# Low parts of seven weight units per layer on GpSimd, centring in another order, and gate tiles at a later place in a two-layer encoder kernel

## The chip, the cores and the metric

The kernel runs on one core of one Trainium2 chip. The metric is the device time of one execution in microseconds, the median of several runs.

## What is computed

A bidirectional encoder trunk of two layers over 256 tokens and 16 learned meta tokens of width 1024, in float32. Each layer projects the normalised tokens with one wide matrix, runs two token mixers on the parts, gates and mixes them, and ends in a squared-ReLU MLP:

```python
h = concat(meta_tokens, x)                                # 272 x 1024
for l in range(2):
    u = rms_norm(h, norm_mix_pre[l])
    q_r, k_r, v_r, g_r, q_a, k_a, v_a, gate_r, gate_a = split(u @ w_in[l])
    y_r = retention_branch(q_r, k_r, v_r, g_r, log_decay) @ w_ret_o[l]   # 8 heads, both directions
    y_a = attention_branch(q_a, k_a, v_a, attn_sink[l]) @ w_att_o[l]     # 8 query heads, 2 key heads
    mix = (sigmoid(gate_r) * y_r + sigmoid(gate_a) * y_a) @ w_mix_o[l]
    h = h + rms_norm(mix, norm_mix_post[l])
    u = rms_norm(h, norm_ff_pre[l])
    h = h + rms_norm(square(relu(u @ w_ff1[l])) @ w_ff2[l], norm_ff_post[l])
return h[:, 16:]
```

## The kernel before

The tokens lie along the free axis, 272 columns in layer 0 and 256 for most of layer 1. The weights come as 130 units per layer, each a tile `raw` of 128 x 1024 float32 loaded by one DMA on the SP queue into a ring of three buffers. `unit()` splits each one: ScalarE (ACT) writes the high part `wh` (L131, a copy to fp32r) and VectorE (DVE) the low part `wl = raw - wh` (L132). Both are kept in rings of four, so a unit is split some units before it is used. `mm3` (L136 to L138) then makes three fp32r matmuls for every 128 x 128 block: wh with the high part of the tokens, wh with their low part, wl with the high part. A unit is 24 matmuls, of some 126 ns each at 272 columns.

Units 4 to 18 of a layer bring the retention values v_r, one head each, the attention's key k_a, four q_a, v_a, and the first of the retention's q_r and k_r. In order: k_a is unit 6 in layer 0 (v_r of head 5 in layer 1), v_r of heads 6 and 7 are 8 and 10, v_a is 12, the four q_a lie at odd numbers around them, q_r and k_r at 14 to 18.

For each value head `value_r` has DVE scale the projection into `vt` (L424). GpSimd (POOL) copies the 16 meta tokens, four times over, into `pads` (L427), and later `centre()` runs on TensorE (PE): one matmul of `pads` for the meta tokens (L430, into `ps_s`) and two of `vt` for the 256 tokens (L432, into `ps_t`). These are deferred and so lie among the matmuls of the next unit. The attention's queries are rotated on DVE (L389 to L392, tile `t`), split into `qa` by ACT (L459) and DVE (L93), and in layer 0 their meta tokens are scaled into a block matrix on POOL (L465, tile `m`), from which L564 takes the meta scores. The values of the attention are copied into `vblk` by POOL (L484) and transposed on PE (L487, L488). Probabilities are scaled by POOL for the meta keys (L594, `pmk`) and by ACT for the others (`pn`, L596).

The retention heads come later in the layer. `similar(hh)` makes two score tiles per head (L680, L681) and multiplies them by the decay `tt` into `sd` (DVE); `retained(hh)` multiplies these with the values (L691) and the meta tokens' state (L692). `meta(t)` makes the `tmx` and `tm` tiles that L692 reads. Behind the first head DVE makes the gate tiles `gt` from `tg` in eight instructions (L720, L721).

Every engine works through its own queue in order. Which instruction comes when on a queue is set by the tile framework's scheduler, from the program's order and its own estimates; `tc.issue_after` adds a constraint that an instruction is issued behind a named one. A small helper records all `scalar_tensor_tensor` instructions, so these carry its line, L93. PE's queue is filled by a list of units (`fill`), with the rest placed between.

Of the kernel before, what the change touches and what calls it, by code (L numbers as in the profile page):

```python
# [22 lines left out]
T = SEQ + NM  # L23
# [4 lines left out]
UNITS = 46 + 4 + 8 + 8 + 32 + 32  # L28
TW = 400
ROW = 320  # L30
LAG = 4
F = [8, 9, 6, 6, 2, 7, 2, 5, 4]
BEHIND = 4
# [8 lines left out]
def encoder(ctx: ExitStack, tc: tile.TileContext, order, w, h_in, gains, dec, decm, sink, sinkm, tabs, mats, esel, masks, rel, relm, grow, out):  # L42
    nc = tc.nc
    V, A, PE, G = nc.vector, nc.scalar, nc.tensor, nc.gpsimd
    mul, add, sub, mn = ALU.mult, ALU.add, ALU.subtract, ALU.min
# [15 lines left out]
    def slot(i, name, shape=(KD, T), dt=F32):  # L61
        return big.tile([P] + list(shape), dt, tag=f"b{i}", name=name)
# [7 lines left out]
    def tokens(i, name, shape=(KD,), at=32):  # L70
        return slot(i, name, (*shape, ROW), F32R)[..., at:at + T]

    def bank(tag, shape=None):
        t = psum.tile([P, 512], F32, tag=tag, name="ps_" + tag, bufs=BANKS[tag])
        if shape is None:
            return t
        n = int(np.prod(shape))
        v = t[:, :n]
        if len(shape) == 2:
            v = v.rearrange("p (a b) -> p a b", a=shape[0])  # L80
        elif len(shape) == 3:
            v = v.rearrange("p (a b c) -> p a b c", a=shape[0], b=shape[1])
        return v
# [5 lines left out]
    def f(t):  # L89
        return t.bitcast(F32)  # L90

    def stt(o, a, s, b, op0=mul, op1=mul):
        V.scalar_tensor_tensor(out=o, in0=a, scalar=s, in1=b, op0=op0, op1=op1)  # L93

    def split(xh, xl, x):
        A.activation(xh, x, AF.Copy)  # L96
# [11 lines left out]
    def fetch(parts=1):  # L108
        i = count["load"]
        count["load"] += 1  # L110
        raw = ring.tile([P, D], F32, tag="raw", name="raw", bufs=3)
        n = D // parts
        cuts = [slice(j * n, (j + 1) * n) for j in range(parts)]
        raws.append((raw, cuts))
        for c in cuts:
            nc.sync.dma_start(raw[:, c], w[i][:, c])
            yield

    def unit(*name):
        i = len(order)  # L120
        order.append(name)
        if not raws:
            list(fetch())
        raw, cuts = raws.pop(0)
        wh = ring.tile([P, D], F32R, tag="wh", name="wh")
        wl = ring.tile([P, D], F32R, tag="wl", name="wl")
        for c in cuts:
            with ExitStack() as later:
                for ins in held.get(i, ()):
                    later.enter_context(tc.issue_after(ins))  # L130
                A.activation(wh[:, c], raw[:, c], AF.Copy)  # L131
                V.tensor_tensor(out=wl[:, c], in0=raw[:, c], in1=f(wh[:, c]), op=sub)  # L132
        return wh, wl

    def mm3(ps, ah, al, bh, bl, first=True, last=True):
        PE.matmul(ps, ah, bh, start=first, stop=False)  # L136
        PE.matmul(ps, ah, bl, start=False, stop=False)  # L137
        return PE.matmul(ps, al, bh, start=False, stop=last)  # L138
# [3 lines left out]
    def flush():  # L142
        while deferred:
            deferred.pop(0)()

    def product(x, c0, tag, *name):
        wh, wl = unit(*name)
        ps = bank(tag, [T])
        for k in range(KD):
            sl = slice(k * P, (k + 1) * P)  # L150
            ins = mm3(ps[:, c0:], wh[:, sl], wl[:, sl], x[0][:, k, c0:], x[1][:, k, c0:], k == 0, k == KD - 1)
            if k == LAG and deferred:
                with tc.issue_after(ins.ins):
# [3 lines left out]
    def proj(x, c0, tag, *name):  # L157
        for _, ps in product(x, c0, tag, *name):
            pass
        return ps  # L160
# [164 lines left out]
    mat = {}  # L325
# [12 lines left out]
    def fourfold(x):  # L338
        return x.unsqueeze(1).to_broadcast([x.shape[0], 4, 16])
# [23 lines left out]
    for l in range(DEPTH):  # L363
        c0 = 16 * l
# [51 lines left out]
        def value_r(hh):  # L416
            q, m = hh // 4, hh % 4
            if m == 0:
                tpv[q] = bank("s", [4, P]), [bank("t") for _ in range(2)]
            tpm, tps = tpv[q]  # L420
            vt = ready.get(hh)
            if vt is None:
                vt = two.tile([P, T], F32, tag="t1", name="vt")
                last = V.scalar_tensor_tensor(out=vt, in0=early.pop(0) if early else proj(u, 0, "a", "v_r", hh), scalar=-0.5, in1=rb, op0=mul, op1=mul)  # L424
                scaled.append(last.ins)
            mine = vtm[:, m]
            G.tensor_copy(mine[:, :, 16 * (m % 2):16 * (m % 2) + 16], fourfold(vt[:, 0:16]))  # L427

            def centre():
                PE.matmul(tpm[:, m], mine, mat["cen"], start=True, stop=True)  # L430
                for c in range(2):
                    PE.matmul(tps[c][:, m * P:(m + 1) * P], vt[:, 16 + c * P:16 + (c + 1) * P], mat["cen"], start=True, stop=True)  # L432
                if m == 3:
                    for c in range(2):
                        A.activation(vr[:, c, q * 512:(q + 1) * 512], tps[c], AF.Copy)
                    A.activation(vm[:, 4 * q:4 * q + 4], tpm, AF.Copy)
                    for r in odds:
                        low = vm[r, 4 * q:4 * q + 4]
                        V.tensor_tensor(out=low, in0=tpm[r], in1=f(low), op=sub)

            deferred.append(centre)
            if early:
                flush()
# [55 lines left out]
        gt = slot(4, "gt")  # L499
# [47 lines left out]
        def behind():  # L547
            return tc.issue_after(anchor[0])
# [12 lines left out]
        if l == 0:  # L561
            ps = bank("s")
# [5 lines left out]
            for c in range(4):  # L568
                V.tensor_tensor(
                    out=pmblk.rearrange("p (t c g k) -> p t c g k", t=4, c=4, g=2)[:, :, c],  # L570
                    in0=mat["blk"].rearrange("p (t g k) -> p t g k", t=4, g=2),
                    in1=pm[:, 0:16].unsqueeze(1).unsqueeze(1).to_broadcast([P, 4, 2, 16]),
                    op=mul,
# [72 lines left out]
        tg = slot(8, "tg")  # L646
# [21 lines left out]
        def similar(hh):  # L668
            gg, t = hh % 2, hh // 2
            tt = two.tile([P, TW], F32, tag="tt", name="tt")  # L670
            tb = two.tile([P, P], F32, tag="tb", name="tb")
            A.activation(tt[:, 144:], rel_sb[:, 0, 144:], AF.Exp, scale=de[:, l, 0, hh:hh + 1])
            A.activation(tt[:, :144], rel_sb[:, 1, :144], AF.Exp, scale=de[:, l, 1, hh:hh + 1])
            A.activation(tb, rel_sb[:, 1, 144:144 + P], AF.Exp, scale=de[:, l, 1, hh:hh + 1])
            V.tensor_tensor(out=tt[:, 144:144 + P], in0=tt[:, 144:144 + P], in1=tb, op=mul)
            sds[hh] = []
            for c in range(2):
                ps = bank("s")
                sl = slice(16 + c * P, 16 + (c + 1) * P)
                PE.matmul(ps[:, c0:T], qk[1][:, gg, t, sl], qk[0][:, gg, t, c0:], start=True, stop=False)  # L680
                PE.matmul(ps[:, c0:T], qk[1][:, gg, t, sl], ql[gg][:, t, c0:], start=False, stop=True)  # L681
                sd = four.tile([P, T], F32, tag="sd", name="sd")
                o = c0 + P - P * c
                stt(sd[:, c0:], ps[:, c0:T], 0.125, tt[:, o:o + T - c0])
                sds[hh].append(sd)

        def retained(hh):
            t = hh // 2
            po = pos[hh] = bank("ot"[hh % 2], [T])
            for c in range(2):  # L690
                PE.matmul(po[:, c0:], vr[:, c, hh * P:(hh + 1) * P], sds[hh][c][:, c0:], start=c == 0, stop=False)  # L691
            PE.matmul(po[:, c0:], vm[:, hh], tm[:, t, c0:], start=False, stop=True)  # L692
            pvs[hh] = square(po[:, c0:], c0)
# [19 lines left out]
        for hh in range(8):  # L713
            with behind():
                if hh < 7:
                    similar(hh + 1)
                retained(hh)
            fill(F[7])
            if hh == 0:
                for m in range(KD):  # L720
                    stt(gt[:, m, c0:], tg[:, m, c0:], 1.0, gt[:, m, c0:], op0=add)  # L721
                rh, rl = tokens(7, "rh", at=32 - c0), tokens(8, "rl", at=32 - c0)
            if hh % 2 and hh < 7:
                with behind():
                    meta((hh + 1) // 2)
            fill(F[6])
            with behind():
                last = normed(hh)
            fill(F[5])
# [9 lines left out]
        for m2 in range(4):  # L739
            wh, wl = unit("att_o", m2)  # L740
            for i in range(2):
                m = 2 * m2 + i
                ps = bank(wide(), [T])
# [6 lines left out]
        for m in range(KD):  # L750
            ps = proj((rh, rl), c0, wide(), "ret_o", m)
# [26 lines left out]
        for m in range(KF):  # L778
            if m % KD == 0:
                a, b = ((5, 7), (8, 9), (6, 10), (2, 3))[m // KD]  # L780
                low = [tokens(i, "fl", (4,), 32 - c0) for i in ("10a", "10b")] if b == 10 else [tokens(b, "fl", at=32 - c0)]
                fs.append((rows(tokens(a, "fh", at=32 - c0)), sum(map(rows, low), [])))
            ps = proj(u, c0, wide(), "ff1", m)
# [203 lines left out]
```

## Time and profile before

| | us |
|---|---|
| median of 3 runs | 874.89 (874.73 to 875.85) |
| the profiled execution | 875.95 |
| its span | 874.2 |
| PE busy | 855.0 (98%) |
| DVE busy | 604.2 (69%) |
| ACT busy | 558.6 (64%) |
| POOL busy | 57.7 (7%) |

The rows are those of one profiled execution. Times are microseconds from the start of the span; busy times are sums over the span. PE's clock was granted in full throughout. An engine that is busy 98% sets the time unless the rest of its idle time is removed, so the rows to look for are those that say what PE waited for. Idle time of another engine costs nothing by itself.

### The profile page before, as it was taken

To read this page: it belongs to the slowest core of one execution; us is meant where nothing else is said; L and a number is where in the kernel's file an instruction comes from. 1 tells how busy PE (TensorE), PEld (TensorE's weight loads), DVE (VectorE), ACT (ScalarE), POOL (GpSimd) and SP (SyncE) were. 2 spreads that over 40 slices of the span, in tenths; PEclk is the share of its full clock that TensorE was granted. 3 is DMA by queue.
4 is the path that set the end of the run, shared out by engine and by line. 5 is a ranking of instruction groups with operands and counts; after the bars stand their busy time and mean duration, and the time that the engine had idled before them with its cause. 6 is when DMAs were issued, how large, how long until landed. Compare 5 with 4: busy or idle time off the path is not lost.

```text
span 874.2 us, 16673 instructions
## 1 busy us (share of the span) xinstructions
PE 855.0 (98%) x6514; PEld 821.9 (94%) x6514; DVE 604.2 (69%) x1113; ACT 558.6 (64%) x1034; POOL 57.7 (7%) x113
## 2 busy tenths in 40 slices
PE   9999999999999999999999999999999999999997
PEld 9899999999989999999988999999999999998885
DVE  6789788767768555444458899888777766554544
ACT  7448887666557777543445578886756598783432
POOL 2123220000000000000001033200000000000000
PEclk9999999999999999999999999999999999999999
DMA  8544344354645655566544444444457476666661
GB/s 293 168 151 127 119 133 136 112 165 154 182 147 164 189 170 177 171 178 183 172 142 144 129 139 146 145 145 122 145 169 212 115 214 208 194 199 194 189 193 70
DMA packets 41407, 142.15 MB, mean 163 GB/s; under 512 B 5360, under 2 KB 6256, under 8 KB 41328
## 3 DMA queue, kind: packets, MB, share of 16 engines
q1 hardware_dynamic: 40896, 140.43, 52.4%
q8 instruction: 51, 0.84, 0.4%
q10 hardware_dynamic: 432, 0.66, 0.3%
q14 instruction: 28, 0.23, 0.1%
HBM read 140.02 MB, written 1.05 MB: 161 GB/s over the span
## 4 chain that ended last, share of the span: by engine, by line
PE 81%; DVE 10%; ACT 6%; issue 1%; POOL 1%; DMA 0%; DVEq 0%; ACTq 0%; POOLq 0%; SPq 0%
PE ps_a L136 12%; PE ps_a L137 12%; PE ps_a L138 12%; PE ps_s L136 5%; PE ps_s L137 5%; PE ps_s L138 5%; PE ps_t L136 4%; PE ps_t L137 4%; PE ps_t L138 4%; DVE wl L132 3%; PE ps_s L848 2%; PE ps_a L848 2%; PE ps_s L847 2%; PE ps_a L847 2%; PE ps_a L849 2%; PE ps_s L849 2%
## 5 line engine op out<-in xcount | busy, mean ns | idle before, releaser
L132 DVE TENSOR_TENSOR wl<-raw,wh 128x1024 fp32r<-128x1024 f32 x256 | 312.8, 1224 | 203.1 <-ACT wh L131 201.4
L131 ACT ACTIVATE wh<-raw 128x1024 fp32r<-128x1024 f32 x256 | 270.0, 1058 | 202.6 <-PE ps_a L137 62.0
L136 PE MATMUL ps_a<-uh,wh 128*128 128x272 f32 (+1 forms) x912 | 266.0, 292 | 2.8 <-ACT uh L242 2.8
L137 PE MATMUL ps_a<-ul,wh 128*128 128x272 f32 (+1 forms) x912 | 259.7, 285 | 0.0
L138 PE MATMUL ps_a<-uh,wl 128*128 128x272 f32 (+1 forms) x912 | 259.7, 285 | 0.0
L136 PEld LDWEIGHTS ps_a<-uh,wh 128*128 128x128 f32 x912 | 171.8, 188 | 4.4 <-ACT uh L242 3.2
L137 PEld LDWEIGHTS ps_a<-ul,wh 128*128 128x128 f32 x912 | 171.7, 188 | 1.0
L138 PEld LDWEIGHTS ps_a<-uh,wl 128*128 128x128 f32 x912 | 171.5, 188 | 0.5 <-DVE wl L132 0.4
L138 PE MATMUL ps_s<-uh,wl 128*128 128x272 f32 (+1 forms) x184 | 52.2, 284 | 0.3 <-DVE wl L132 0.3
L137 PE MATMUL ps_s<-ul,wh 128*128 128x272 f32 (+1 forms) x184 | 52.4, 285 | 0.0
L136 PE MATMUL ps_s<-uh,wh 128*128 128x272 f32 (+1 forms) x184 | 52.3, 285 | 0.0
L136 PE MATMUL ps_t<-uh,wh 128*128 128x272 f32 (+1 forms) x152 | 43.4, 285 | 1.3 <-ACT uh L242 1.3
L137 PE MATMUL ps_t<-ul,wh 128*128 128x272 f32 (+1 forms) x152 | 43.3, 285 | 0.0
L138 PE MATMUL ps_t<-uh,wl 128*128 128x272 f32 (+1 forms) x152 | 43.0, 283 | 0.0
L138 PEld LDWEIGHTS ps_s<-uh,wl 128*128 128x128 f32 x184 | 34.6, 188 | 0.5 <-DVE wl L132 0.5
L136 PEld LDWEIGHTS ps_s<-uh,wh 128*128 128x128 f32 x184 | 34.9, 189 | 0.0
L137 PEld LDWEIGHTS ps_s<-ul,wh 128*128 128x128 f32 x184 | 34.8, 189 | 0.0
L136 PEld LDWEIGHTS ps_t<-uh,wh 128*128 128x128 f32 x152 | 28.5, 188 | 1.5 <-ACT uh L242 1.5
L137 PEld LDWEIGHTS ps_t<-ul,wh 128*128 128x128 f32 x152 | 28.5, 188 | 0.1
L138 PEld LDWEIGHTS ps_t<-uh,wl 128*128 128x128 f32 x152 | 28.5, 188 | 0.0
L97 DVE TENSOR_TENSOR fl<-ft,fh 128x272 fp32r<-128x272 f32 (+1 forms) x64 | 27.6, 432 | 1.0 <-ACT fh L96 0.9
L96 ACT ACTIVATE fh<-ft 128x272 fp32r<-128x272 f32 (+1 forms) x64 | 27.1, 424 | 1.7
(308 smaller groups left out, 1955.2 us busy)
## 6 DMA issues: line engine op xcount, KB each, us to landing
raw<-in_w SPq DMA_DIRECT2D x256, 512.0 KB, 3.7
leads<-in_w SPq DMA_DIRECT2D x6, 256.0 KB, 5.5
tab<-in_tabs SPq DMA_DIRECT2D x2, 544.0 KB, 6.3
h<-in_h_in SPq DMA_DIRECT2D x3, 272.0 KB, 5.8
out<-yt SPq DMA_DIRECT2D x3, 256.0 KB, 2.1
leads<-in_w ACTq DMA_DIRECT2D x2, 256.0 KB, 3.6
gj<-in_grow SPq DMA_DIRECT2D x1, 512.0 KB, 5.4
mats<-in_mats SPq DMA_DIRECT2D x1, 320.0 KB, 7.2
```

What stands on the lines that cost most here:

```text
L96: A.activation(xh, x, AF.Copy)
L97: V.tensor_tensor(out=xl, in0=x, in1=f(xh), op=sub)
L131: A.activation(wh[:, c], raw[:, c], AF.Copy)
L132: V.tensor_tensor(out=wl[:, c], in0=raw[:, c], in1=f(wh[:, c]), op=sub)
L136: PE.matmul(ps, ah, bh, start=first, stop=False)
L137: PE.matmul(ps, ah, bl, start=False, stop=False)
L138: return PE.matmul(ps, al, bh, start=False, stop=last)
L847: PE.matmul(pss[i], xh, wh[:, sl], start=kk == 0, stop=False)
L848: PE.matmul(pss[i], xh, wl[:, sl], start=False, stop=False)
L849: PE.matmul(pss[i], xl, wh[:, sl], start=False, stop=kk == KF - 1)
```

## The change

Three edits. The subtraction that makes `wl` goes to GpSimd for the seven units 6, 8, ..., 18 of each layer. In `centre()` the two token matmuls come before the meta matmul. The eight gate instructions behind head 0 are issued after the last `sd` of `similar(1)`; for this `stt` and `similar` return the instruction.

```diff
+ON_POOL = range(6, 19, 2)
...
     def stt(o, a, s, b, op0=mul, op1=mul):
-        V.scalar_tensor_tensor(out=o, in0=a, scalar=s, in1=b, op0=op0, op1=op1)
+        return V.scalar_tensor_tensor(out=o, in0=a, scalar=s, in1=b, op0=op0, op1=op1)
...
                 A.activation(wh[:, c], raw[:, c], AF.Copy)
-                V.tensor_tensor(out=wl[:, c], in0=raw[:, c], in1=f(wh[:, c]), op=sub)
+                (G if i % UNITS in ON_POOL else V).tensor_tensor(out=wl[:, c], in0=raw[:, c], in1=f(wh[:, c]), op=sub)
...
             def centre():
-                PE.matmul(tpm[:, m], mine, mat["cen"], start=True, stop=True)
                 for c in range(2):
                     PE.matmul(tps[c][:, m * P:(m + 1) * P], vt[:, 16 + c * P:16 + (c + 1) * P], mat["cen"], start=True, stop=True)
+                PE.matmul(tpm[:, m], mine, mat["cen"], start=True, stop=True)
...
-                stt(sd[:, c0:], ps[:, c0:T], 0.125, tt[:, o:o + T - c0])
+                last = stt(sd[:, c0:], ps[:, c0:T], 0.125, tt[:, o:o + T - c0])
                 sds[hh].append(sd)
+            return last
...
-                    similar(hh + 1)
+                    last = similar(hh + 1)
...
                 for m in range(KD):
-                    stt(gt[:, m, c0:], tg[:, m, c0:], 1.0, gt[:, m, c0:], op0=add)
+                    with tc.issue_after(last.ins):
+                        stt(gt[:, m, c0:], tg[:, m, c0:], 1.0, gt[:, m, c0:], op0=add)
```

The new lines shift the numbers: L132 is L133 in the changed kernel, L427 is L428, L484 is L485, and the helper's L93 is L94.

On POOL's queue in layer 0, from the fill of the block matrix `m` on. The names are `vt` of the successive heads, `t2` for rotated queries, `vat` for the attention's values. Before:

```order
L406 MEMSET m0_383 128x512 [waits DVE_49,Activation_49,Pool_49]
L427 COPY pads_355<-vt_392 128x4x16 [waits DVE_49]
L427 COPY pads_355<-vt_398 128x4x16 [waits DVE_49]
L427 COPY pads_355<-vt5_324 128x4x16 [waits DVE_49,PE_49]
L427 COPY pads_355<-vt_404 128x4x16 [waits DVE_49]
L427 COPY pads_355<-vt_410 128x4x16 [waits DVE_49]
L427 COPY pads_355<-vt_424 128x4x16 [waits DVE_49]
L465 ISA
L465 TENSOR_SCALAR m0_383<-t2_510 64x16 [waits DVE_49]
L465 TENSOR_SCALAR m0_383<-t2_510 64x16 [waits Pool_49]
L427 COPY pads_355<-vt_521 128x4x16 [waits DVE_49,Pool_49]
```

After, with the rows between the first copy and the last of the six left out and the queue followed to the subtraction of unit 16:

```order
L133 ISA
L133 TENSOR_TENSOR wl_430<-raw_113,wh_429 128x1024 [waits DMAHW0_49,PE_49,Activation_49]
L428 COPY pads_355<-vt_392 128x4x16 [waits DVE_49]
...
L133 TENSOR_TENSOR wl_525<-raw_522,wh_524 128x1024 [waits DMAHW4_49,Activation_49]
L133 TENSOR_TENSOR wl_605<-raw_602,wh_604 128x1024 [waits DMAHW6_49,PE_49,Activation_49]
...
L428 COPY pads_355<-vt_521 128x4x16 [waits DVE_49,Pool_49]
L133 TENSOR_TENSOR wl_689<-raw_686,wh_688 128x1024 [waits DMAHW0_49,PE_49,Activation_49]
...
L485 COPY vblk_123<-vat_388 64x4x16 [waits DVE_49]
L485 COPY vblk_123<-vat_388 64x4x16 [waits Pool_49]
L133 TENSOR_TENSOR wl_947<-raw_944,wh_946 128x1024 [waits PE_49,DMAHW4_49,Activation_49,Pool_49]
```

The library instruction (ISA) moves with the first long instruction to the front, and subtractions stand between the copies. The subtraction of unit 12 is right behind the copy for head 6, and that of unit 16 behind the copies into `vblk`.

On the same queue in layer 1, before:

```order
L427 COPY pads_5862<-vt_5873 128x4x16
L427 COPY pads_5862<-vt_5879 128x4x16
L427 COPY pads_5862<-vt_5885 128x4x16
L427 COPY pads_5862<-vt_5891 128x4x16
L427 COPY pads_5862<-vt_5905 128x4x16
L427 COPY pads_5862<-vt_5956 128x4x16
L427 COPY pads_5862<-vt_6034 128x4x16
L427 COPY pads_5862<-vt_6112 128x4x16
L484 COPY vblk_123<-vat_5869 64x4x16 x2
L594 TENSOR_SCALAR pmk_6308<-ex_6315,rs_6312 128x4x16
```

After:

```order
L428 COPY pads_5862<-vt_5873 128x4x16
L428 COPY pads_5862<-vt_5879 128x4x16
L133 TENSOR_TENSOR wl_6038<-raw_6035,wh_6037 128x1024
L428 COPY pads_5862<-vt_5885 128x4x16
L428 COPY pads_5862<-vt_5891 128x4x16
...
L428 COPY pads_5862<-vt_6112 128x4x16
L133 TENSOR_TENSOR wl_6292<-raw_6289,wh_6291 128x1024
L133 TENSOR_TENSOR wl_6431<-raw_6428,wh_6430 128x1024
L485 COPY vblk_123<-vat_5869 64x4x16 x2
L595 TENSOR_SCALAR pmk_6308<-ex_6315,rs_6312 128x4x16
```

The subtraction of unit 8 now stands ahead of the copies of the third and fourth heads, and that of unit 16 ahead of the copies into `vblk`, the other way round than in layer 0.

On DVE's queue in layer 1, where the gate tiles are made. Before:

```order
L93 SCALAR_TENSOR_TENSOR sd<-ps_s,tt 128x256 [waits PE_49] x2
L93 SCALAR_TENSOR_TENSOR gt<-tg,gt 128x256 [waits Activation_49]
L93 SCALAR_TENSOR_TENSOR gt<-tg,gt 128x256 x4
L93 SCALAR_TENSOR_TENSOR tmx<-ps_s,tmx 128x256 [waits PE_49]
L93 SCALAR_TENSOR_TENSOR gt<-tg,gt 128x256
L93 SCALAR_TENSOR_TENSOR thr<-ps_a,rb 128x256 [waits PE_49]
L93 SCALAR_TENSOR_TENSOR sd<-ps_s,tt 128x256 [waits DVE_49,PE_49]
L93 SCALAR_TENSOR_TENSOR sd<-ps_s,tt 128x256 [waits PE_49]
L664 TENSOR_TENSOR tm<-tmx,tm 64x256 [waits Activation_49]
L93 SCALAR_TENSOR_TENSOR gt<-tg,gt 128x256 x2
```

After:

```order
L94 SCALAR_TENSOR_TENSOR sd<-ps_s,tt 128x256 [waits PE_49] x2
L94 SCALAR_TENSOR_TENSOR tmx<-ps_s,tmx 128x256 [waits PE_49]
L676 TENSOR_TENSOR tt<-tt,tb 128x128 [waits Activation_49]
L94 SCALAR_TENSOR_TENSOR thr<-ps_a,rb 128x256 [waits PE_49]
L665 TENSOR_TENSOR tm<-tmx,tm 64x256 [waits Activation_49]
L94 SCALAR_TENSOR_TENSOR sd<-ps_s,tt 128x256 [waits PE_49] x2
L94 SCALAR_TENSOR_TENSOR gt<-tg,gt 128x256 x8
```

The eight `gt` are one block behind the second head's `sd`; `tmx` follows the first head's `sd` directly, and a `tt` that waits for ACT comes between `tmx` and `tm`. On PE L692, which reads `tm`, stands five matmuls earlier among those of the weight unit.

## Rows read from the trace of the kernel before

**Rows 1.** The page, busy us, share of the span, and instructions of each engine.
```profile
PE 855.0 (98%) x6514; PEld 821.9 (94%) x6514; DVE 604.2 (69%) x1113; ACT 558.6 (64%) x1034; POOL 57.7 (7%) x113
```

**Rows 2.** PE's waits: line, awaited engine, tile and line; total us, times, longest.
```profile
PE ps_s L430 <- POOL pads L427: 2.6, 4, 0.8
PE ps_s L680 <- DVE tmx L93: 1.2, 1, 1.2
PE ps_t L432 <- DVE vt L424: 1.1, 1, 1.1
PE ps_t L603 <- ACT pn L596: 0.9, 1, 0.9
```

**Rows 3.** The page's costliest groups: busy us, mean ns; idle before, releaser.
```profile
L132 DVE TENSOR_TENSOR wl<-raw,wh 128x1024 fp32r<-128x1024 f32 x256 | 312.8, 1224 | 203.1 <-ACT wh L131 201.4
```

**Rows 4.** Single lines of POOL: duration in ns, minimum/median/maximum; first and last start.
```profile
L329 POOL MEMSET kblk<- x3: 525/525/525, 0.7 to 1.6; 128x512 f32 x3
L329 POOL MEMSET ql<- x1: 1007/1007/1007, 2.8 to 2.8; 128x1088 f32 x1
L465 POOL TENSOR_SCALAR m<-t x8: 248/251/536, 40.2 to 62.1; 64x16 f32<-64x16 f32 x8
L594 POOL TENSOR_SCALAR pmk<-ex,rs x32: 435/446/2393, 68.5 to 558.8; 128x64 f32<-128x64 f32 x32
L427 POOL COPY pads<-vt x16: 237/272/1295, 23.4 to 498.2; 128x64 f32<-128x64 f32 x16
```

**Rows 5.** Timeline near 525 us: start, duration, instruction, [idle before, releaser].
```profile
524.71 2.34 DVE L132 TENSOR_TENSOR wl<-raw,wh 128x1024 fp32r<-128x1024 f32 x2
524.89 2.39 POOL L594 TENSOR_SCALAR pmk<-ex,rs 128x64 f32<-128x64 f32 x1 [0.32 <-DVE rs L557]
```

**Rows 6.** Timeline of POOL and DVE, layer 0, 57 to 62 us.
```profile
57.21 1.56 POOL L484 COPY vblk<-vat 64x64 f32<-64x64 f32 x2 [6.45 <-DVE vat L93]
61.81 0.56 POOL L465 TENSOR_SCALAR m<-t 64x16 f32<-64x16 f32 x2 [2.08 <-DVE t L392]
...
57.41 1.26 DVE L132 TENSOR_TENSOR wl<-raw,wh 128x1024 fp32r<-128x1024 f32 x1
58.70 0.90 DVE L93 SCALAR_TENSOR_TENSOR qa<-t,qa 64x272 fp32r<-64x272 f32 x2
```

**Rows 7.** Timeline, layer 0, first centring, 18 to 30 us.
```profile
18.39 0.53 POOL L406 MEMSET m<- 128x512 f32 x1 [13.57 <-DVE ss L261]
20.72 1.04 ACT L131 ACTIVATE wh<-raw 128x1024 fp32r<-128x1024 f32 x1
29.51 0.37 PE L138 MATMUL ps_a<-uh,wl 128*128 128x272 f32 x1
```

**Rows 8.** Timeline, layer 0, 40 to 47 us.
```profile
40.19 0.59 POOL L465 TENSOR_SCALAR m<-t 64x16 f32<-64x16 f32 x2 [7.90 <-DVE t L392]
45.03 0.49 PE L430 MATMUL ps_s<-mats,pads 128*128 128x128 f32 x2 [0.74 <-POOL pads L427]
46.41 0.44 DVE L389 TENSOR_TENSOR t<-ps_a,tab 128x272 f32<-128x272 f32 x1 [1.53 <-PE ps_a L138]
```

**Rows 9.** Timeline, layer 1, first centring, 475 to 479 us.
```profile
475.30 1.06 ACT L131 ACTIVATE wh<-raw 128x1024 fp32r<-128x1024 f32 x1 [1.74 <-DMA raw<-in_w]
478.45 0.38 PE L136 MATMUL ps_a<-uh,wh 128*128 128x272 f32 x1
```

**Rows 10.** Timeline, layer 1, copies into vblk and their transpose.
```profile
503.99 1.06 ACT L131 ACTIVATE wh<-raw 128x1024 fp32r<-128x1024 f32 x1 [1.93 <-PE ps_a L137]
505.20 1.54 POOL L484 COPY vblk<-vat 64x64 f32<-64x64 f32 x2 [6.53 <-DVE vat L93]
506.81 0.32 PE L488 MATMUL ps_t<-mats,vblk 128*128 128x128 f32 x1
```

**Rows 11.** Timeline, layer 1, gate tiles and the retained product.
```profile
573.47 1.77 DVE L93 SCALAR_TENSOR_TENSOR gt<-tg,gt 128x256 f32<-128x256 f32 x5 [0.93 <-ACT tg L647]
577.41 0.37 PE L692 MATMUL ps_o<-tm,vm 128*128 128x256 f32 x1
```

## The prediction

> **What bounds the kernel now.** The page's busy times come first: TensorE (PE) is busy 98% of the span, DVE 69%, GpSimd (POOL) 7% [rows 1]. PE is the bound, so an edit is worth what it takes from PE's idle time, and work moved off DVE is worth nothing by itself. The view of PE's waits comes next. Four of its rows lie where the change works: L430, the centring of the meta tokens, waits for POOL's copies into pads 2.6 us in four places; L680 waits 1.2 us for tmx; L432 1.1 us for vt; L603 0.9 us for pn [rows 2]. That is 5.8 us, 0.7% of the span, and nothing that the change does can gain more than this and a few tenths. The rest of the working is how much of it comes back, and what the GpSimd instructions put in front of PE instead. All sums are made against the profiled execution, 875.95 us, of which 874.2 us is span. It lies 1.06 us above the median of the runs, 874.89 us, so 1.06 is taken off at the end.
>
> **Price of the moved instruction.** Fourteen wl subtractions of 1.224 us leave DVE [rows 3]: 17.1 us, worth nothing on their own. The trace of before holds no two-input GpSimd instruction of 128x1024, so its time X is bounded. A fill takes 525 ns for 512 elements a partition and 1007 ns for 1088 [rows 4], so (1007-525)/576 = 0.84 ns an element and about 0.1 us fixed. One element for each such step gives X = 0.96 us, the low end. The TENSOR_SCALAR takes 248 ns for 16 elements and 435 ns for 64 [rows 4], 3.9 ns an element; at that rate X = 0.25 + 1008 x 3.9 ns = 4.2 us, the high end. A subtraction of two tiles has no scalar to fetch, and its form is nearer to the copy, 237 ns for 64 elements [rows 4]: two reads of 0.84 ns give 1024 x 1.68 + 0.1 = 1.82, taken as **X = 1.85 us**, 0.6 more than on DVE.
>
> The Trainium skill, GPSIMD Engine Reference, § 3.1 on elementwise work, gives 4497 ns for 2048 fp32 elements; half of it is 2.25 us, an estimate, and by it the sum below would end at 879.4 instead of 877.4. No run here shows this instruction yet.
>
> **Do the two engines hold each other up?** A POOL instruction that takes 435 ns at the least took 2393 ns while DVE ran two wl, which read two SBUF tiles each [rows 4, 5]: it ended only with them. Two copies of some 0.27 us took 1.56 us across a wl, which itself took 1.26 instead of 1.224 us [rows 6]. So DVE surely blocks POOL. That POOL blocks DVE is not shown at length, since no long POOL instruction reads SBUF in this trace. I take it as mutual: a wl on POOL keeps every DVE instruction with two SBUF inputs waiting for X.
>
> The Trainium skill, SBUF — State Buffer, § Who interferes with whom, says the same of a pair of ports shared as an exclusive lock, which whoever comes first holds for the whole instruction. This speaks against the change. The row of 2393 ns agrees for one direction; the other is what the second rival turns on.
>
> **Layer 0, first centring.** wh of unit 6 ends at 20.72 + 1.04 = 21.76 [rows 7]. The subtraction comes before all six pads copies on POOL, behind a library instruction that can begin after the fill at 18.39 + 0.53 [rows 7]. What that costs has one bound: at the place where it stands before, POOL idled 7.90 us [rows 8], so 0 to 7.9 us. The middle, 4 us, puts the subtraction at 22.9 to 24.75. The copies still come in time, and the meta matmuls, now behind the token matmuls, wait for the last copy alone, which no longer stands behind a wl of unit 7, as that moved behind vt. PE goes back to weight units at about 28.6 instead of 29.51 [rows 7]: +0.9 (from -1.0 with the full 7.9 to +1.2).
>
> **Layer 0, 42 to 62 us.** Before, PE waits 1.1 us for vt of head 6, which stands behind qa on DVE, and then 0.74 for the copy [rows 2, 8]. After, vt is ahead of qa, and the tokens' centring covers the copy: 1.84 more, so PE could be 2.74 ahead here. But from here the rotations of q_a lead, on DVE. With the 0.9 from the start, vt of head 6 ends at about 42.5 and its copy at 42.95; the subtraction of unit 12 stands right behind it on POOL, 42.95 to 44.8, and qa, two instructions of 0.45 with two SBUF inputs, waits: 45.7. The next rotation started at 46.41 before, when DVE had idled 1.53 us for PE [rows 8], so 0.7 is left of the 2.74. The subtractions of units 14 and 16 do the same: each holds 1.85 where a wl of 1.224 stood, 1.26 for both. The one of 16 stands between the copies of vblk and the query's TENSOR_SCALARs that L564 needs, and on DVE qa, at 58.70 before, waits for its end [rows 6]. The TENSOR_SCALARs, at 61.81 before [rows 6], come 1.26 - 0.7 = 0.56 late, and PE with them. **Layer 0: -0.5** (a loss), between +2.74 if POOL holds nothing up and -4.2 if a subtraction waits for a wl besides (below).
>
> **Layer 1, centring.** wh of unit 8 runs from 475.30 to 476.36 and had waited for its DMA [rows 9], so an earlier PE does not help. Its subtraction now stands ahead of the copies of vt 2 and 3. It ends at 478.2, copies and last matmuls take about 0.5 each, and PE is back at 479.2, against 478.45 [rows 9]: **-0.7**, whether or not the engines share a lock.
>
> **Layer 1, vblk.** wh of unit 16 ends at 505.05, 0.1 before vat is there for the copies of vblk [rows 10]. The subtraction stands ahead of them, to 506.9. The copies took 1.54 us before, sharing time with DVE [rows 10]; qa, which waited, competes again, so the same is taken: 508.4, and L488, at 506.81 before [rows 10], starts **1.6** later. With copies of 0.27 us it is 0.6.
>
> **The gate tiles.** Before, tmx stands behind five gt of 1.77 us together [rows 11], and L680 waits 1.2 us [rows 2]. After, all eight gt stand behind the next head's sd, so that wait goes. What is late next is tm: on DVE a tt that waits for ScalarE's exponentials now stands between tmx and tm, and L692, at 577.41 before [rows 11], has moved five matmuls forward and waits for tm. I leave 0.1 of the 1.2 in layer 1 and give 0.2 to layer 0, where the same wait is short: **+0.3** (0 to +1.4).
>
> **Sum.** -0.5 - 0.7 - 1.6 + 0.3 = -2.5: 875.95 + 2.5 - 1.06 = **877.4 us**, 0.3% slower. The other moved subtractions have no copy behind them on POOL that PE is near to. I cost them at nothing: wh and wl are made ahead in rings of four, and that cover is gone only if a subtraction comes more than a unit late; then L138 waits for it. A raw buffer also comes free 0.6 us later each time; where wh waits for its load, as at 475.30 [rows 9], that can cost as much, inside the range.
>
> **Rivals.**
> First, POOL doesn't hold DVE up (**other side, faster**). For it: DVE's 1.26 us wl beside the copies [rows 6] lost 0.04 only. Then layer 0 keeps 2.74, layer 1 loses 0.7 + 0.6, the gates give 0.3: +1.7, so 873.2; with X = 0.96 both losses of layer 1 go and with the gates' full 1.4 it is 870.5. It decides by whether qa at 44.8 and 55 to 60 starts inside a subtraction.
> Second, half and half: most DVE instructions in a rotation read PSUM or one tile and slip past, and only qa is held. Layer 0 then gives about half, 1.4; layer 1 as just told: 1.4 - 1.3 + 0.3 = +0.4, 874.5, no change.
> Third, POOL is starved: each subtraction also waits for a wl, as the row of 2393 ns did [rows 5], so 3.07 us. Layer 0: 46.9 instead of 45.7 is 0.5 late, and 2 x 1.85 more, -4.2; layer 1 -1.9 and -2.85; with the gates -8.65: 883.5. Against it: ScalarE and DMA leave DVE gaps in both places.
>
> **How the numbers follow.** Forecast 0.38, no hold on DVE 0.32, half and half 0.18, starved 0.12. A measurement of this kernel can tell about 0.2%, 1.75 us, from no change. Of the second case 0.26 lies below 873.1, the rest within; the half case is within but for 0.02 on each side; of the forecast 0.04 is within. So faster 0.28, same 0.26, slower 0.46, rounded. The range goes from 871.5, which leaves out the best of the faster case (0.05), to 881.0, which takes in X = 2.25 and leaves out the starved case (0.12).
>
> **What would show it.** Right: GpSimd subtractions near 1.85 us; PE's wait for pads gone in layer 0 but new waits of L430 for pads near 478 us and of L488 for vblk near 507; qa on DVE starting where a subtraction ends; L692 waiting for tm. Wrong: subtractions over 2.5 us or under 1.2; qa starting inside a subtraction; PE more than 1 us ahead of before at 62 us, in which case the gain of layer 0 stays and the first rival holds.

## The result, and the profile after

The changed kernel takes 885.3 us (median of 4 runs, 883.0 to 886.86), the kernel before 875.37 us (4 runs in the same comparison): 1.0093 of before, 95% interval 1.0072 to 1.0114. The change makes the kernel slower, as forecast, but by about four times as much (+9.9 us against the forecast's +2.5) and beyond the range, which ended at 881.0.

The profiled execution of the changed kernel took 883.94 us with a span of 882.1 us, 7.9 us more than before. What follows accounts for this execution; two of the four runs took 886.66 and 886.86 us, nearly 3 us more than it, and no trace here shows why. The page's part 1 (busy us, share, instructions):

```profile
PE 857.1 (97%) x6514; PEld 823.5 (93%) x6514; DVE 604.4 (69%) x1099; ACT 559.7 (63%) x1034; POOL 82.6 (9%) x127
```

The page's group of the moved instruction (busy us, mean ns, idle before and what ended it):

```profile
L133 POOL TENSOR_TENSOR wl<-raw,wh 128x1024 fp32r<-128x1024 f32 x14 | 34.1, 2434 | 39.1 <-DVE wl L133 21.3 <-ACT wh L132 17.8
```

GpSimd's (POOL's) 14 subtractions take 2.43 us each, against 1.224 on DVE [rows 3]. DVE lost 14 instructions and is as busy as before [rows 1]: 604.4 us. What it no longer spends on subtractions it spends waiting inside other instructions, and a wait inside an instruction counts as busy: where GpSimd fills instead of subtracting (an experiment below), DVE is busy for 588.5 us. TensorE's (PE's) busy time rose by 2.1 us for the same 6514 matmuls. The view of PE's waits, to be read against [rows 2]:

```profile
PE ps_t L604 <- ACT pn L597: 3.2, 3, 1.8
PE ps_t L432 <- DVE vt L425: 2.9, 2, 2.3
...
PE ps_s L565 <- POOL m L466: 1.9, 1, 1.9
PE ps_s L433 <- POOL pads L428: 1.5, 2, 1.3
...
PE ps_t L489 <- POOL vblk L485: 1.3, 1, 1.3
...
PE ps_o L694 <- DVE tm L665: 0.8, 1, 0.8
```

Two of the four waits of before have shrunk or gone: pads from 2.6 to 1.5 us, tmx altogether. Those for m, vblk and tm are new; pn has grown from 0.9 to 3.2 us and vt from 1.1 to 2.9. The wait for wl is 0.3 us in both kernels: that the moved low parts are ready later costs PE nothing directly.

To see where the time went, the start of the same matmul is compared in both traces, counted from PE's first. PE's order differs by a few places at the moved instructions, so each figure holds to some tenths of a microsecond.

| place (start of the matmul before) | after, us later | without units 16 and 18 | fills in place of subtractions | orders alone |
|---|---|---|---|---|
| 40.9, layer 0, after the first centring | -1.9 | -1.2 | -1.3 | -1.3 |
| 58.3, ahead of vblk's transpose | 0.0 | -1.0 | -3.4 | -1.7 |
| 68.8, behind the meta scores (L564) | +2.0 | -0.1 | -3.8 | -1.6 |
| 138.2, behind attention and gates | +4.6 | -0.5 | -4.5 | -2.0 |
| 468.3, layer 1, ahead of the first centring | +4.6 | -0.5 | -4.5 | -2.0 |
| 480.3, behind it | +5.4 | +0.3 | -4.8 | -3.6 |
| 509.1, behind vblk's transpose | +6.8 | +0.4 | -4.4 | -3.5 |
| 549.1, inside the attention | +8.3 | +0.8 | -4.5 | -3.0 |
| 579.4, behind the gates | +7.9 | +0.5 | -4.9 | -3.3 |

The three right-hand columns are experiments, told below. Of the -1.9 in the first row, 0.6 stands already at 10.5 us, ahead of every edit; in the other columns the place at 10.5 us is within 0.1 of before. From there to 40.9 us each of the four gains 1.3 to 1.4. Behind 579.4 us the two kernels run alike. The timeline of PE at that last place, of before and of after (the numbering of lines moves by two):

```profile
579.45 0.59 PE L697 MATMUL ps_t<-sq,mats 128*128 128x256 f32 x2
```

```profile
587.40 0.59 PE L699 MATMUL ps_t<-sq,mats 128*128 128x256 f32 x2
```

**Who holds whom.** The timelines of POOL and of DVE after the change, four places together: a start, a duration, the instruction.

```profile
30.38 2.40 POOL L133 TENSOR_TENSOR wl<-raw,wh 128x1024 fp32r<-128x1024 f32 x1 [2.09 <-ACT wh L132]
34.73 2.39 POOL L133 TENSOR_TENSOR wl<-raw,wh 128x1024 fp32r<-128x1024 f32 x1 [1.95 <-ACT wh L132]
58.33 2.46 POOL L133 TENSOR_TENSOR wl<-raw,wh 128x1024 fp32r<-128x1024 f32 x1
68.80 2.39 POOL L133 TENSOR_TENSOR wl<-raw,wh 128x1024 fp32r<-128x1024 f32 x1 [4.46 <-ACT wh L132]
...
31.28 2.58 DVE L133 TENSOR_TENSOR wl<-raw,wh 128x1024 fp32r<-128x1024 f32 x1
35.35 2.07 DVE L393 TENSOR_TENSOR t<-t,t 128x272 f32<-128x272 f32 x1
59.05 2.52 DVE L94 SCALAR_TENSOR_TENSOR qa<-t,qa 64x272 fp32r<-64x272 f32 x2 [0.50 <-ACT qa L460]
68.92 3.02 DVE L570 TENSOR_TENSOR m<-mats,m 128x128 f32<-128x128 f32 x4
```

Each DVE row has its partner. The subtraction of 34.73 ends at 37.12; the sum t<-t,t of two SBUF tiles, 0.44 us elsewhere, starts beside it at 35.35 and takes 2.07, to 37.42. The two qa that took 0.90 [rows 6] take 2.52 and end at 61.57, 0.78 behind the subtraction's end at 60.79. The four small products m<-mats,m, together 0.89 before, take 3.02:

```profile
66.97 0.89 DVE L569 TENSOR_TENSOR m<-mats,m 128x128 f32<-128x128 f32 x4
```

An instruction that reads one tile from PSUM and one from SBUF keeps its 0.44 us beside a subtraction (L392 at 34.88). That GpSimd holds DVE, which no row of before could show, is so.

The Trainium skill, SBUF — State Buffer, § Who interferes with whom, calls the ports that the two engines share an exclusive lock, and says that a DVE instruction with two SBUF inputs contends with a GpSimd instruction that reads SBUF. These rows agree for the direction that was open, 2.07 us for a sum of 0.44; the row of 2393 ns agrees for the other [rows 4, 5].

**The clock.** PE's waits do not make up the whole loss. The stretches' rows after the change (length, busy times of PE, PEld, DVE, ACT, POOL with counts, then PE's granted clock):

```profile
44.00:46.00 2.00, 2.00 (x11) 2.00 (x10) 0.00 (x0) 0.06 (x1) 1.79 (x1) 0.50 0.34 139
...
74.00:76.00 2.00, 2.00 (x10) 2.00 (x10) 0.77 (x2) 1.90 (x5) 0.41 (x2) 0.50 0.06 25
```

The clock is 0.50, the lower level of 1.2 GHz, behind PE's waits of 2.3 us at 40 to 42.5 and of 1.8 us at 71 to 73: PE makes 10 or 11 matmuls in 2 us, where 18 are usual at 1.00. Before, the clock read 1.00 at both places and fell only at 870.8 us, behind the last matmul. Against before PE fell back by 1.3 us in the first stretch and by 1.5 in the second; behind the second, 0.9 was made good by 136 us, since PE then waited less.

### The profile page after: what moved, and what is told of

It reads as the page before. It is cut to its first block, busy times and chain, and to the rows that moved or that the text cites. A ratio compares the mean times of both kernels' runs of the same rounds, so it can differ in the third digit from the quotient of the medians.

```text
span 882.1 us, 16668 instructions
## 1 busy us (share of the span) xinstructions
PE 857.1 (97%) x6514; PEld 823.5 (93%) x6514; DVE 604.4 (69%) x1099; ACT 559.7 (63%) x1034; POOL 82.6 (9%) x127
## 4 chain that ended last, share of the span: by engine, by line
PE 80%; DVE 10%; ACT 6%; issue 2%; DMA 1%; POOL 0%; SPq 0%; DVEq 0%; ACTq 0%
PE ps_a L137 12%; PE ps_a L138 12%; PE ps_a L139 12%; PE ps_s L139 5%; PE ps_s L138 5%; PE ps_s L137 5%; PE ps_t L137 4%; PE ps_t L138 4%; PE ps_t L139 4%; DVE wl L133 3%; ACT wh L132 2%; PE ps_a L851 2%; PE ps_s L851 2%; PE ps_s L850 2%; PE ps_a L850 2%
## 5 line engine op out<-in xcount | busy, mean ns | idle before, releaser
L133 DVE TENSOR_TENSOR wl<-raw,wh 128x1024 fp32r<-128x1024 f32 x242 | 297.4, 1231 | 199.5 <-ACT wh L132 198.0
L132 ACT ACTIVATE wh<-raw 128x1024 fp32r<-128x1024 f32 x256 | 269.7, 1058 | 198.0 <-PE ps_a L138 59.6
L133 POOL TENSOR_TENSOR wl<-raw,wh 128x1024 fp32r<-128x1024 f32 x14 | 34.1, 2434 | 39.1 <-DVE wl L133 21.3
L499 POOL MEMSET ql<- 64x1088 f32 x2 | 2.0, 1001 | 319.4 <-PE ps_s L138 319.3
```

Of the source, the lines that this page charges most:

```text
L133: (G if i % UNITS in ON_POOL else V).tensor_tensor(out=wl[:, c], in0=raw[:, c], in1=f(wh[:, c]), op=sub)
L499: nc.gpsimd.memset(f(ql[0][halves[1]]), 0.0)
```

## The experiments

The theory, lock: while a GpSimd subtraction reads two tiles, no DVE instruction with two SBUF inputs runs, and this is what costs. The rivals: queue (short GpSimd copies stand behind long subtractions), order (the new places of the centring and the gates), and sums (each subtraction costs alike). The experiments ran in three groups, each on a chip of its own with the kernel before beside it (pool alone, orders alone, without 18 and fills on one; centring alone, gates alone, only 6 and quarters on the next; the rest on the third). So a kernel is compared by its ratio to before on its own chip, and by the profiled executions' start of the matmul at 579.4 us of before (the last row of the table), called **mark** below. In the profiled executions of five kernels (without 18, gates alone, only 6, quarters, without 8 and 10) matmuls of layer 1's MLP, far behind every edit, took 118 ns instead of 113 without a wait and at clock 1.00, 3 to 5 us in all; this is left out by the mark. The mark is of one execution, and the half-clock stretches, of up to 1.5 us, are in it: where mark and ratio differ, both are given, and a difference of less than some 1.5 us in the mark alone says little.

**Only the moved subtractions** (centring and gates as before):

```diff
+                PE.matmul(tpm[:, m], mine, mat["cen"], start=True, stop=True)
                 for c in range(2):
                     PE.matmul(tps[c][:, m * P:(m + 1) * P], ...)
-                PE.matmul(tpm[:, m], mine, mat["cen"], start=True, stop=True)
...
-                    with tc.issue_after(last.ins):
-                        stt(gt[:, m, c0:], tg[:, m, c0:], 1.0, gt[:, m, c0:], op0=add)
+                    stt(gt[:, m, c0:], tg[:, m, c0:], 1.0, gt[:, m, c0:], op0=add)
```

> Only the moved subtractions; centring and gate tiles as before the change. Theory, lock: each subtraction of 2.4 us on GpSimd holds DVE's instructions with two SBUF inputs, and this is where the time goes; then this kernel is as slow as the changed one or slower, 884 to 888 us, and DVE rows of 2 us and more stand beside GpSimd's subtractions. Rival, order: the centring's and gates' new places cost a good part; then 878 to 881.

Measured: 883.13 us, 1.0043 of before (1.0028 to 1.0058); mark +6.9. A little under lock's range and above the rival's: the loss comes without the new orders. How much of it is less sure. By the mark it is 6.9 of the 7.9 us, by the ratio 0.43% against the change's 0.93%; the kernel before ran between 874.42 and 881.48 us on this chip. Against the kernel with the orders alone (next), on the same chip, this one is 8.5 us slower.

Two of its subtractions took longer than any in the changed kernel, 3.37 and 3.22 us. POOL's and DVE's timelines at the first:

```profile
35.13 3.37 POOL L133 TENSOR_TENSOR wl<-raw,wh 128x1024 fp32r<-128x1024 f32 x1
...
34.99 1.25 DVE L133 TENSOR_TENSOR wl<-raw,wh 128x1024 fp32r<-128x1024 f32 x1
```

The wl on DVE came first and ends at 36.24; the subtraction ends 2.26 us behind it. So DVE can hold up GpSimd's subtraction as well.

**Only the new orders:**

```diff
-ON_POOL = range(6, 19, 2)
+ON_POOL = ()
```

> Only the new order of the centring and the new place of the gate tiles; all subtractions on DVE. Lock: 873 to 875, the waits for pads mostly gone, tmx's wait of 1.2 us replaced by one for tm of up to 1. Rival, order: 878 or more.

Measured: 874.62 us, 0.9943 (0.9922 to 0.9964); mark -3.3. As lock had it, the two orders are a gain: PE's wait for pads is left at one place (1.0 us), and tm's wait of 0.9 us has taken the place of tmx's, as expected.

**The centring alone**, and **the gates alone** (the same edit, with the one or the other order undone as above):

> Only the new order of the centring. If the 3.3 us that both orders together gained come from it: 871.5 to 873 us by the clock of the first runs, 0.994 to 0.997 of before; PE waits 1.2 us for tmx as before. Rival: the scheduler's other shifts made the gain; then 0.999 or more.

Measured: 875.17 us, 0.9973 (0.9954 to 0.9993); mark -2.6. The ratio lies a little above the range; the rival had 0.999 or more.

> Only the new place of the gate tiles. The wait for tmx (1.2 us) goes and a wait for tm of 0.8 to 0.9 us comes, at a matmul that now stands earlier: -0.3 to +0.2 us, no change, 0.998 to 1.002 of before. Rival: the wait removed is a gain of 1 us, 0.9985 or less, with no wait for tm.

Measured: 874.64 us, 0.9986 (0.9964 to 1.0008); mark -0.1, no change, as expected. By the mark the centring makes most of the gain; the gates' new place trades tmx's wait for tm's 0.8 us. The mark of -0.1 is a sum, though: PE fell back by 1.5 us in a half-clock stretch from 46 us on (0.52 at 46 to 48), behind waits of 1.4 us for vt and 0.7 for pads, with no subtraction on GpSimd, and came forward by 1.4 in the first centring of layer 1, for a reason that is not shown. At the gates themselves it gained 0.4, as the changed kernel did.

**Fills in place of the subtractions:**

```diff
-                (G if i % UNITS in ON_POOL else V).tensor_tensor(out=wl[:, c], in0=raw[:, c], in1=f(wh[:, c]), op=sub)
+                if i % UNITS in ON_POOL:
+                    G.tensor_copy(wl[:, 0:16], f(wh[:, 0:16]))
+                    for n in (D, D, 288):
+                        G.memset(f(wl[:, 0:n]), 0.0)
+                else:
+                    V.tensor_tensor(out=wl[:, c], in0=raw[:, c], in1=f(wh[:, c]), op=sub)
```

> The changed kernel, but GpSimd's subtractions are replaced by a copy of 16 elements from wh and three fills of the wl tile, 2.4 us together, which read nothing; the low part of these units is left out of the result. GpSimd is as busy and its copies queue as before. Lock, of reads: DVE isn't held, no DVE row of over 2 us beside GpSimd's fills, and PE's waits for m near 64 us and pn near 73 us go: 876 to 879. Rival, queue: within 1.5 us of the changed kernel. Between (a lock of writes too): DVE held as before.

Measured: 873.77 us, 0.9952 (0.9931 to 0.9974); mark -4.9, so 12.9 us earlier than the changed kernel by the mark, and faster than lock's range. GpSimd is as busy, 82.7 us against 82.6. Its timeline and DVE's at the place of the four products:

```profile
63.30 1.96 POOL L136 MEMSET wl<- 128x1024 f32 x2
...
63.19 0.90 DVE L575 TENSOR_TENSOR m<-mats,m 128x128 f32<-128x128 f32 x4
```

Beside a fill the products take their 0.90 us. So at this place it isn't GpSimd's queue or its busy time that costs, but its reading. Two things differ besides: the fills come in pieces, between which the scheduler put some copies, and a raw buffer comes free as soon as wh is made. Both may have helped elsewhere, the pieces above all where a copy stood behind a whole subtraction; neither shortens a DVE instruction. By the mark the kernel ends 1.6 us below the orders alone; whether this is the relief of DVE is not shown, and the times, 873.77 and 874.62 us, don't tell the two apart.

The Trainium skill, SBUF — State Buffer, § Who interferes with whom, says that a DVE instruction with two SBUF inputs doesn't contend with a GpSimd instruction that only writes SBUF; the 0.90 us agree.

**Without unit 18**, **without 16 and 18**, **without 8 and 10** (`ON_POOL` without these numbers):

> The changed kernel with the subtraction of unit 18 back on DVE in both layers. Lock: the four small mask products that took 3.02 us beside it in layer 0 fall to about 0.9, PE's wait of 1.8 us for pn near 73 us goes, and with it the stretch at half the granted clock behind it, 1.3 us or so: 880.5 to 882 in place of 884 to 885. Rival, queue: what costs is short GpSimd copies queued behind subtractions; behind this one PE waits for none, so under 0.7 us comes back.

Measured: 880.2 us, 1.003 (1.0003 to 1.0056); mark +4.0, 3.9 less than the changed kernel; the rival had under 0.7. The four products take 0.28 us each again, as the view of their line shows (minimum/median/maximum in ns):

```profile
L570 DVE TENSOR_TENSOR m<-mats,m x4: 280/283/284, 69.2 to 69.8; 128x128 f32<-128x128 f32 x4
```

And of PE's waits there:

```profile
PE ps_t L604 <- ACT pn L597: 0.9, 1, 0.9
```

The wait of 1.8 us in layer 0 is gone, and the clock at 74 to 76 us reads 1.00; what is left of pn is the 0.9 us of before [rows 2].

> The changed kernel with the subtractions of units 16 and 18 back on DVE. Lock: the waits for m (1.9 us), for pn (1.8 us) and in layer 1 for vblk (1.3 us) go, and the half-clock stretch near 75 us: 5.5 to 7 us faster than the changed kernel, 1.000 to 1.003 of before; what is left is 1.3 us for pads in layer 1 and the stall at 42 us. Rival, sums: 2/7 of the loss, 2.3 us: 1.006 to 1.007.

Measured: 878.53 us, 1.0019 (1.0006 to 1.0033); mark +0.5. By the mark two of seven subtractions per layer carry 7.5 of the 7.9 us, by the ratio 0.74 of the 0.93%. Of the 7.5, 1.0 stands in the table already at 58.3 us, ahead of unit 16's subtraction, and is the clock's: at 44 to 46 us, behind a wait of PE's of 2.1 us for vt, it was full here, against 0.50 in the changed kernel behind 2.3 us. In the kernel without unit 18 it was 0.50 behind a wait of 2.1 us as well, so the length of the wait doesn't tell the two apart. The stretch in this kernel, and in the one without 18:

```profile
44.00:46.00 2.00, 2.00 (x17) 2.00 (x17) 0.61 (x4) 0.63 (x1) 2.00 (x1) 1.00 0.50 195
```

```profile
44.00:46.00 2.00, 2.00 (x10) 2.00 (x10) 0.00 (x0) 0.15 (x1) 2.00 (x1) 0.50 0.48 190
```

> The changed kernel with the subtractions of units 8 and 10 back on DVE. If these two make PE's wait of 2.3 us for vt at 42 us, by holding DVE in k_a's rotation, that wait falls under 1 us and the stretch at half the clock behind it goes. Whether that counts: the later holds (units 12 to 18) still pace DVE to 62 us, so in layer 0 under 1 us is left of it at the wait for m; in layer 1 the wait of 1.3 us for pads goes. Together 1.5 to 3 us faster than the changed kernel, 1.004 to 1.007 of before. Rival, sums: each subtraction costs the same; then 2/7 of the loss of 8, 2.3 us, spread over both places.

Measured: 884.46 us, 1.0107 (1.0069 to 1.0146); mark +8.6. A miss: taking these two away is no gain. In layer 1 the wait for pads did go, and the first centring cost 1.5 us less than in the changed kernel; but in layer 0, 2.2 us were lost by 58.3 us. The scheduler now puts unit 12's subtraction ahead of the queries' scaling and of the copy into pads, and PE waits for that copy. POOL's timeline, and PE's:

```profile
41.69 2.60 POOL L133 TENSOR_TENSOR wl<-raw,wh 128x1024 fp32r<-128x1024 f32 x1 [12.55 <-DVE kal L452]
44.26 0.91 POOL L466 TENSOR_SCALAR m<-t 64x16 f32<-64x16 f32 x2
45.23 0.24 POOL L428 COPY pads<-vt 128x64 f32<-128x64 f32 x1
...
45.52 0.80 PE L433 MATMUL ps_s<-mats,pads 128*128 128x128 f32 x2 [2.33 <-POOL pads L428]
```

Here the queue costs, 2.33 us. So queue is a second mechanism, not merely a rival, and sums is out: taking two units away gives 7.5, taking two others less than nothing, since what a subtraction costs hangs on what stands beside and behind it.

**Only unit 6 on GpSimd:**

> The changed kernel with the subtraction of unit 6 alone on GpSimd in each layer, both new orders kept. Lock: beside it stands little that DVE has to do with two SBUF inputs in layer 0; in layer 1 it stands across the making of rb and vt, so 0.5 to 0.7 us are lost there: 0.995 to 0.997 of before, close to the kernel with the orders alone. Rival: GpSimd's slow subtraction delays its own unit or the copies behind it: 0.999 or more.

Measured: 874.29 us, 0.9969 (0.9953 to 0.9985); mark -3.1, as the orders alone (-3.3). Where DVE has little with two SBUF inputs to do, a subtraction on GpSimd costs nothing that can be told here; it gains nothing either.

**Subtractions in quarters:**

```diff
+                    for s in (slice(256 * n, 256 * n + 256) for n in range(4)):
+                        G.tensor_tensor(out=wl[:, s], in0=raw[:, s], in1=f(wh[:, s]), op=sub)
```

> The changed kernel with each of GpSimd's subtractions cut into four of 256 columns. If the hold lasts for one instruction of GpSimd, DVE gets in between the quarters: no two-input DVE instruction waits for more than about 0.7 us on one, the waits for m near 64 us and for pn near 73 us shrink from 1.9 and 1.8 to 0.7 or less, and the kernel is 3 us or more faster than the changed one, 876 to 880, 0.998 to 1.004 of before. Rival, throughput: the engines share one reader, so the same 2.4 us of reading delay DVE by the same sum: 1.007 or more. GpSimd's own finish is later in either case, since DVE gets in as well.

Measured: 876.08 us, 0.9995 (0.998 to 1.0011); mark -0.1, 8.0 us earlier than the changed kernel. The time is as expected, but only one of the two waits shrank, m's, from 1.9 to 0.2 us; pn's stays at 1.7:

```profile
PE ps_t L608 <- ACT pn L601: 2.8, 3, 1.7
...
PE ps_s L569 <- POOL m L470: 0.2, 1, 0.2
```

The timelines show why, at the four products:

```profile
64.12 2.95 POOL L135 TENSOR_TENSOR wl<-raw,wh 128x256 fp32r<-128x256 f32 x4 [4.45 <-ACT wh L132]
...
64.25 2.97 DVE L574 TENSOR_TENSOR m<-mats,m 128x128 f32<-128x128 f32 x4
```

Four products and four quarters take turns, one of each (the products take 0.75 to 0.82 us instead of 0.28), and the products together take as long as beside a whole subtraction. The hold is per instruction: cutting it helps one waiting DVE instruction, and does not help a row of as many as there are pieces.

**Towards a better version.** With all subtractions on DVE, the third head's decay tile behind tm on ACT and DVE:

```diff
+            with ExitStack() as later:
+                if hh == 2:
+                    later.enter_context(tc.issue_after(tms[0]))
+                    later.enter_context(tc.issue_after(tma[0]))
```

> Both new orders without the moved subtractions, and the decay tile of the third head is made behind tm. The wait of 0.9 us for tm is then gone if ScalarE's decay instructions ahead of tm's copy made it: 0.5 to 0.9 us faster than the orders alone, 0.993 to 0.996 of before. Rival: tm's copy now stands behind a wh, so the wait stays within 0.3 us of what it was.

Measured: 873.43 us, 0.9966 (0.9946 to 0.9986); mark -3.9. The ratio lies just above the range, and tm's wait fell from 0.9 to 0.6 us only, since tm's copy now stands behind a wh: nearer the rival. The 0.6 us by the mark are too few to count.

And with the copies into pads on ACT (`A.activation(..., AF.Copy)` for `G.tensor_copy`):

> As the one before, and the copies into pads are made by ScalarE, which no lock touches, in place of GpSimd. PE's wait of 1.0 us for pads near 43 us shrinks if the copy was late because a wl on DVE held it; the gain is 0.5 to 1 us, 0.992 to 0.995 of before. Rival: the copy waits behind a wh or the qa instructions on ScalarE, and the wait stays or grows: 0.997 or more.

Measured: 873.28 us, 0.9973 (0.9961 to 0.9985); mark -3.0. The rival holds: PE now waits 1.2 us for ACT's copies and 1.0 for vt. The versions with the new orders and without GpSimd's subtractions lie at 0.994 to 0.997 of before, ahead of both kernels, and their intervals don't tell them apart.

## Why the prediction was wrong

**The direction and the mechanism** were right: POOL holds DVE up, and this turns a gain into a loss. The first rival (no hold) is refuted by the rows of 2.07 and 2.52 us, and by the fills. Its gain was real, though: with fills, which read nothing, the forecast's +1.7 us came as 4.9 by the mark, 3.3 of it from the orders alone. The second rival was right that an instruction which reads PSUM slips past, and wrong that only qa is held: t<-t,t and m<-mats,m are held too, and its 874.5 us is 10.8 below the measured time.

**The price X.** Taken as 1.85 us, between 0.96 and 4.2; it is 2.40 (2.35 to 2.69 over the 14). Two reads at the fill's rate were too cheap. With the working otherwise as it stood, X = 2.40 makes qa, behind unit 12, end at 42.95 + 2.40 + 0.90 = 46.25, 0.16 ahead of before, and the holds of units 14 and 16 cost 2 x (2.40 - 1.224) = 2.35, so m comes 2.2 us late instead of 0.56. Measured at that place: 2.0. For units 14 and 16 the mechanism was right there and X too small: qa waits for the end of each. For unit 12 the agreement is luck: its subtraction started at 43.15, behind the first qa, and held nothing; the next rotation started at 46.12 all the same, since it waited for PE, which ran at half clock.

The Trainium skill, GPSIMD Engine Reference, § 3.1, whose figure gave an estimate of 2.25 us, was nearer than my rows: 2.40 measured, 7% above it.

**Unit 18: the step that failed.** "The other moved subtractions have no copy behind them on POOL that PE is near to. I cost them at nothing." I looked at what is queued behind a subtraction on its own engine and not at what runs beside it on DVE, though that was my own mechanism. Unit 18's stands across the four products of two SBUF tiles, from which pn's chain goes to PE. It costs 2.6 us in layer 0 (+2.0 to +4.6 in the table: 2.0 at PE's wait, 1.5 by the clock, less the 0.9 that came back), and 1.5 in layer 1 (+6.8 to +8.3; the kernel without it goes from +4.3 to +4.4 there). In layer 1 it held t<-t,t, which took 1.37 us; by what steps that reached PE no run shows. The kernel without it gives 3.9 back.

**The first centring and 42 us.** The centring gave 1.3 us instead of 0.9, and PE came to it 0.6 ahead by no edit of the change. The vt of head 6 ended at 42.51, as forecast (42.5); but PE had come so much earlier that it waited 2.3 us for it, and then ran at half the clock. The forecast had the 2.74 us eaten on DVE by 62 us; it was eaten by 48, with the clock, which had no place in the sum, taking 1.3 of it. Why the clock fell here, and in the kernel without 18, and not in the kernel without 16 and 18, behind nearly the same wait, is open.

**Layer 1.** The centring cost 0.85 (forecast 0.7), vblk 1.4 (forecast 1.6); PE's new wait for vblk is 1.3. These two were queue's, and were seen. POOL's timeline and PE's at vblk:

```profile
510.55 2.38 POOL L133 TENSOR_TENSOR wl<-raw,wh 128x1024 fp32r<-128x1024 f32 x1 [2.70 <-ACT wh L132]
512.88 0.73 POOL L485 COPY vblk<-vat 64x64 f32<-64x64 f32 x2
...
513.66 0.33 PE L489 MATMUL ps_t<-mats,vblk 128*128 128x128 f32 x1 [1.26 <-POOL vblk L485]
```

That vblk's size came so near is in part luck: the subtraction took 0.53 us more than X, and the copies behind it 0.73 instead of the forecast's 1.5. The gates gave +0.4 (forecast 0.3), with L694 waiting 0.8 us for tm, as told.

**The sum**, by the table: layer 0 -4.6 (forecast -0.5), layer 1's centring and vblk -2.25 (-2.3), unit 18 in layer 1 -1.5 (0), gates +0.4 (+0.3): -7.95 against -2.5. Of the difference of 5.45 us, 1.5 stand at L564's place (X, and at unit 12 the clock), 2.6 are unit 18 in layer 0 with the clock behind it, and 1.5 unit 18 in layer 1, less 0.15 in the other places. Two small sums of the prediction don't come out: by its own terms the best of the first rival is 870.75 and not 870.5 us, and the chances add up to 0.24 for the same and 0.48 for slower. The miss doesn't hang on either.

**The third rival** came nearest in time (883.5) by a mechanism that was not at work here: in the changed kernel GpSimd's subtractions ran 2.35 to 2.69 us; it was DVE that waited. That a subtraction can wait for a wl is so, as the 3.37 and 3.22 us of the kernel with the subtractions alone show.

**The range** had X up to 2.25 in it with the hold on DVE taken at three places only, units 12, 14 and 16 of layer 0; unit 18's two places, and the clock, were in none of its cases.

## What to carry to other kernels

Before work goes from DVE to GpSimd, list for each moved instruction which DVE instructions with two SBUF inputs fall into its span, and follow who waits for them; GpSimd's idle share (93% here) says nothing about it. Where such an instruction lies on a chain to the bound engine, the move can cost nearly GpSimd's whole duration (2.13 us of 2.39 at the four products) and not only the difference of the two prices (1.2); it is the difference where the moved instruction stood in front of the same one before, as at qa. A row of several small ones was hurt as much by four pieces as by one long instruction. An edit that only reorders gained here (0.3 to 0.6%), and the one that shifted 17 us of work lost.

## What the runs showed of the hardware that was not expected

- A GpSimd subtraction of 128x1024 takes 2.35 to 2.69 us in the changed kernel, and 3.37 where a wl on DVE came just before it; in quarters it takes 0.74 us each (median). Filling the same tile takes 0.95.
- DVE instructions that read one of their inputs from PSUM ran at 0.44 us beside it; those with two in SBUF waited up to 2.2 us (t<-t,t, 2.61 us for 0.44). Beside GpSimd's fills the longest t<-t,t took 0.50.
- PE's granted clock fell to 0.50 for about 3 us behind waits of 2.3 and of 1.8 us. At nearly the same place, behind a wait of 2.1 us, it fell in the kernel without 18 and did not fall in the kernel without 16 and 18.
- Matmuls of 256 columns took 118 instead of 113 ns in layer 1's MLP in some executions, at granted clock 1.00; the cause is open.
